# A decoder layer on one core: all units in one chain, a third memory unit in seven products, later pairs of y

## The chip, the cores and the metric

The kernel runs on one core of one Trainium2 chip. The time is device microseconds of one execution, the median of several. The profile is one further execution, taken by the hardware profiler; its rows give times in microseconds from the start of its span. The engines are called PE (TensorE's products), PEld (TensorE's weight loads, which overlap the products), DVE (VectorE), ACT (ScalarE), POOL (GpSimd) and SP (SyncE, which here only issues transfers).

## What is computed

One hybrid decoder layer on 256 tokens of width 2048, in fp32:

```python
h = x
h = h + 0.5 * swiglu(rmsnorm(h), w1_gate, w1_up, w1_down)       # f1, D_FF = 5632
z = rmsnorm(h) @ w_in                                           # q, kv, v, u
y_a = spatial_gating(gelu(z_u), gelu(z_v))                      # chunk 128, 8 groups
y_b = window_attention_sinks(z_q, z_k, z_v)                     # window 128, 16 heads, 2 kv heads
h = h + concat(rmsnorm(y_a), rmsnorm(y_b)) @ w_out              # wo
h = h + cross_attention(rmsnorm(h), rmsnorm(mem), w_xq, w_xkv, w_xo)   # mv0 mv1 mk0 mk1, xq, xo
h = h + 0.5 * swiglu(rmsnorm(h), w2_gate, w2_up, w2_down)       # f2
out = rmsnorm(h)
```

The memory has 256 rows; its projection `w_xkv` has 4096 columns, which four units of 1024 columns compute: mk0 and mk1 (keys) and mv0 and mv1 (values).

## The kernel before

**Products in three passes.** Every fp32 operand a is split into a rounded part ah (type fp32r) and a rest al; a product a.b is then ah.bh + al.bh + ah.bl, three matmuls of 128x128 by 128x512. `split` (L147) does it: ScalarE casts (L148), VectorE subtracts (L149).

**Units and chunks.** A unit is 1024 columns of a weight matrix for all 256 tokens, so its output is four blocks of 128x512 in PSUM. It runs over chunks of 256 rows of the weights; the 256x256 block of the activations that belongs to a chunk is a "pair" (a class `Pair`, L172), transposed, with its gain applied, and split. `load` (L298) issues the transfer of a chunk's weights, 1 MB on SP's queue, into one of three buffers `raw`, and splits them into `wh` and `wl`, of which there are two buffers each. `Unit.multiply` (L349) issues the products (L363).

**Kinds.** A chunk of kind N takes eight block products in three passes, 24 matmuls. A chunk of kind S takes seven by a scheme of the Strassen-Winograd sort, 21 matmuls, and needs sums of the weight blocks (a tile `t`, L310 to L314, split into `th` and `tl`) and sums of the activation blocks (`fill`, L193). Kind C takes 24 with other intermediates, and stands among S chunks in a unit. `KINDS` = "CCSCSCSC" is the order in the gate units and in mv1 and mk0; mv0 and mk1 are eight N chunks. The unit of seven products keeps its partial sums P1, Q6, Q7 in the PSUM pool `trp`, which the transposes also use (four banks); the other sums lie in `acc` (four banks). `seven_early` and `seven_late` (L479, L487) make the four blocks from them. For wo and xo, `KINDS_O` gives the kinds of the pairs and `HALVES_O` the kinds of the chunks in each of the two halves.

**The order.** TensorE's instructions run in the order in which they are traced (`manual_schedule` for PE). The other engines' orders, and which buffer a tile gets and when, are planned by the framework: by the order of tracing as a priority (`high_priority` lifts it), and by when inputs and buffers are ready in the planner's own estimate of time. `push` (L426) traces the load of a chunk, then `flush` (L411) traces the products of the chunk pushed before, and what follows them (`post`: evictions). So a load is traced one chunk ahead of its products. `unit` (L440), `narrow_unit` (L450) and `seven_unit` (L496) end with `flush`, so the next unit's first load is traced behind all of their products and evictions; `gu_unit`, `added_unit` and the down units don't flush within their stage.

**Side work.** Transposes and small products of attention, gating and norms are written as generators. `multiply` calls `side_step` (L389) after every six matmuls; a step runs one ready generator to its next `yield n`, which makes it ready again n steps later. `until` and `have` (L398, L403) run generators at once where a result is needed. Side work is `held` during the S chunks of units that use all four `trp` banks, and spaced by three steps in `sparse` units.

**Stages, in order.** f1: one plain gate unit on x as it is (its rows come transposed from DRAM by `prep1`, L736, one pair per chunk; the norm's factor is applied afterwards), then ten gate units on normalized forms n1, then four down units. Then q, kv, v, u; then mv0, mv1, mk0, mk1; then wo, xq, xo; then f2 with eleven gate units and four down units. The windowed attention (`attend`, L861, two lanes) runs as side work in v, u and mv0, the gating in mv0, the forms of y (`y_pairs`, L976) where `YFORMS` says, counted in finished chunks of mk0 and mk1, and the memory attention (`attend_memory`, L1082) in xq and xo. The pairs of the normalized memory, mT (`pair_normalized`, L252), are made one per chunk of u. `next_norm` (L664) makes the pairs for the next stage out of h; for n4 it scales rows by the factor of the first half first (`scaled`, L690).

**Pools.** `fp` has 14 forms of high and low parts, `tmp` seven tiles of 128x512 (tag `s2`: raw blocks, temporaries), `mid` twelve of 128x1024. An instruction that writes a tile waits until its buffer's last reader is done.

The lines that set the order around the change are:

```python
def push(u, i, w, p, post=None, pieces=None):
    ...
        b = load(u.s, w, u.kinds[i], pieces)
    flush()
    pending.append((u, i, p, b, post))
```

Of the kernel before, what the change touches and what calls it, by code (L numbers as in the profile page):

```python
# [8 lines left out]
F32 = mybir.dt.float32  # L9
# [13 lines left out]
NG = D // 512  # L23

# [6 lines left out]
def layer_kernel(  # L31
# [23 lines left out]
    ctx.enter_context(tc.manual_schedule(engines={mybir.EngineType.PE}))  # L55
# [185 lines left out]
    def pair_from_dram(s, srcT, i, gcol, base=None, raw=None):  # L241
        if raw is None:
            raw = s2(s + "r").rearrange("p (k t) -> p k t", k=2)
            nc.sync.dma_start(raw, srcT[i * T:(i + 1) * T, :].rearrange("(k p) t -> p k t", p=P))
# [7 lines left out]
    def pair_normalized(s, kind, srcT, i, gcol, by_token):  # L252

        raw = s2(s + "r").rearrange("p (k t) -> p k t", k=4)
        src = srcT[i * T:(i + 1) * T, :].rearrange("(k p) t -> p k t", p=P)
        for tb in range(TB):
            a, b = laid(kind, 0, tb), laid(kind, 1, tb)
            nc.gpsimd.dma_start(raw[:, a:b + 1:b - a, :], src[:, :, tb * P:(tb + 1) * P])
        turned = 1 if kind == "S" else 0
# [38 lines left out]
    def load(s, w, kind, pieces):  # L298
# [5 lines left out]
        if kind == "S":  # L304
# [4 lines left out]
            split(wh[:, 1:, :], wl[:, 1:, :], raw[:, 1:, :])  # L309
# [4 lines left out]
            nc.vector.tensor_tensor(t[:, 3, :], t[:, 2, :], raw[:, 3, :], ALU.add)  # L314
            split(th, tl, t)
# [95 lines left out]
    def flush():  # L411
        while pending:
            u, i, p, b, post = pending.pop(0)
            if u.late and all(name in u.left for name in u.late):
                held[0] = u.kinds.index("S") <= i <= u.kinds.rindex("S")
            held[0] = held[0] or i in u.alone
            tight[0] = u.sparse and u.kinds.index("S") <= i <= u.kinds.rindex("S")
            u.multiply(u.kinds[i], p(), b, i in (0, len(u.kinds) - 1))
            held[0] = False
# [4 lines left out]
    emptied = []  # L424

    def push(u, i, w, p, post=None, pieces=None):  # L426
        with ExitStack() as order:
            if emptied:

                order.enter_context(tc.issue_after(emptied.pop().ins))  # L430
            b = load(u.s, w, u.kinds[i], pieces)
        flush()
        pending.append((u, i, p, b, post))
# [3 lines left out]

    BLOCKS = (("P2", 0, 0), ("Q3", 0, 1), ("R", 1, 1), ("Q4", 1, 0))
# [11 lines left out]
    def narrow_unit(s, w, pairs):  # L450

        ps = [acc.tile([P, 512], F32, tag="acc", name=nm(s)) for _ in range(TB)]
        for c in range(2):
# [5 lines left out]
            for k in range(8):  # L459
                p = have(pairs, (c * 8 + k) // 2)  # L460
                side_step()
                for tb in range(TB):
                    hi, lo = p[f"A{tb + 1}{k % 2 + 1}"]
                    for i, (x, y) in enumerate(((hi, wh), (lo, wh), (hi, wl))):
                        nc.tensor.matmul(
                            ps[tb][:, :256], x, y[:, k, :],
                            start=c + k + i == 0, stop=c == 1 and k == 7 and i == 2,
                        )
        return ps

    KINDS = "CCSCSCSC"

    KINDS_O = "NNNSNSSN"
    HALVES_O = ("NNNNNNSN", "NNNSNSNN")
# [798 lines left out]
```

## Time and profile before

| | |
|---|---|
| median of 3 runs | 2106.76 us (2105.95 to 2106.78) |
| profiled execution, its own time | 2105.79 us |
| its span | 2104.0 us |
| granted clock, mean | 0.996 |
| moved by DMA | 402.15 MB, mean 191 GB/s |

The span is what the rows of the trace cover; the profiled execution's time is 1.8 us more. In the head of the page each engine has its busy time, its share of the span and its instructions. PE's products are pipelined and the ends of their rows are modelled, so rows overlap: what a product costs in a dense stretch is the distance from one start to the next. A row of windows gives the length of the stretch, then the busy time and number of instructions of PE, PEld, DVE, ACT and POOL, then the granted clock of TensorE (1.00 is full), the DMA's share and GB/s. A row of waits names who waited, for what, and then total, times and longest. A row of a timeline is start, length, engine, line, operation, output and inputs; in brackets stands the idle time before it and what ended it.

### The profile page before, as it was taken

What the parts mean: (1) busy time and instruction counts of PE and PEld (TensorE: products, weight loads), DVE (VectorE), ACT (ScalarE), POOL (GpSimd) and SP (SyncE); (2) the same over time, 40 slices, a digit from 0 to 9 for tenths busy, and PEclk for the clock granted to TensorE, in tenths of its full rate; (3) what the DMA queues carried; (4) which work ended last, traced back from release to release, by engine and by line L of the source; (5) the groups of instructions that cost most, each with busy time, mean ns of one, the idle gap of its engine ahead of it and who ended that gap; (6) DMA issues with size and microseconds to landing.
All of it is one profiled execution on the core that took longest, in us unless ns stands there. A gap on an engine that the chain in (4) does not pass through costs nothing.

```text
span 2104.0 us, 23815 instructions
## 1 busy us (share of the span) xinstructions
PE 2076.0 (99%) x9527; PEld 1715.5 (82%) x9527; DVE 1674.5 (80%) x1609; ACT 1135.4 (54%) x1109; POOL 32.2 (2%) x51
## 2 busy tenths in 40 slices
PE   9999999999999999999999999999999999999998
PEld 7888888888888888788888888778888888888886
DVE  5888888888987745867858657798888888889878
ACT  7655555555544645544545455665555545555444
POOL 0000000000000000100000000000000000000000
PEclk9999999999999999999999999999999999999999
DMA  7555555555555554435555543455555555555553
GB/s 281 195 189 213 200 195 184 209 188 199 202 199 206 201 210 166 167 140 200 180 180 184 197 160 140 163 197 200 181 207 197 204 191 200 200 200 200 200 198 122
DMA packets 60110, 402.15 MB, mean 191 GB/s; under 512 B 6864, under 2 KB 8928, under 8 KB 12768
## 3 DMA queue, kind: packets, MB, share of 16 engines
q1 hardware_dynamic: 57280, 393.50, 51.7%
q0 software_dynamic: 2016, 6.30, 0.9%
q8 instruction: 74, 1.21, 0.2%
q10 hardware_dynamic: 704, 0.84, 0.1%
q14 instruction: 36, 0.29, 0.0%
HBM read 398.52 MB, written 2.10 MB: 190 GB/s over the span
## 4 chain that ended last, share of the span: by engine, by line
PE 94%; DVE 3%; ACT 1%; issue 1%; DMA 1%; POOL 0%; SPq 0%; POOLq 0%; DVEq 0%; ACTq 0%
PE f2gQ L363 16%; PE f1gQ L363 15%; PE f1dQ L363 6%; PE f2dQ L363 6%; PE f2gP L363 6%; PE f1gP L363 5%; PE f1dP L363 3%; PE f2dP L363 3%; PE woQ L363 2%; PE xqQ L363 2%; PE f1dR L363 2%; PE f2dR L363 2%; PE xoQ L363 2%; PE mk0Q L363 1%; PE mv1Q L363 1%; PE mv0Q L363 1%
## 5 line engine op out<-in xcount | busy, mean ns | idle before, releaser
L149 DVE TENSOR_TENSOR f1gwl<-f1gw,f1gwh 128x2048 fp32r<-128x2048 f32 (+1 forms) x91 | 185.5, 2043 | 51.6 <-ACT f1gwh L148 51.4
L148 ACT CAST f2gwh<-f2gw 128x1536 fp32r<-128x1536 f32 (+1 forms) x88 | 154.4, 1755 | 133.4 <-PE f2gQ L363 96.6
L148 ACT CAST f1gwh<-f1gw 128x2048 fp32r<-128x2048 f32 (+1 forms) x91 | 156.1, 1716 | 123.5 <-PE f1gQ L363 90.4
L149 DVE TENSOR_TENSOR f2gwl<-f2gw,f2gwh 128x1536 fp32r<-128x1536 f32 (+1 forms) x88 | 183.7, 2088 | 40.3 <-ACT f2gwh L148 40.2
L363 PE MATMUL f2gQ<-f2gwh,n4fh 128*128 128x512 f32 x363 | 141.4, 390 | 0.0
L363 PE MATMUL f2gQ<-f2gwh,n4fl 128*128 128x512 f32 x363 | 141.3, 389 | 0.0
L363 PE MATMUL f1gQ<-f1gwh,n1fh 128*128 128x512 f32 x330 | 128.6, 390 | 0.0
L363 PE MATMUL f1gQ<-f1gwh,n1fl 128*128 128x512 f32 x330 | 128.4, 389 | 0.0
L148 ACT CAST f2dwh<-f2dw 128x2048 fp32r<-128x2048 f32 (+1 forms) x44 | 79.2, 1799 | 91.2 <-PE f2dQ L363 71.2
L148 ACT CAST f1dwh<-f1dw 128x2048 fp32r<-128x2048 f32 (+1 forms) x44 | 79.2, 1799 | 87.9 <-PE f1dQ L363 68.2
L149 DVE TENSOR_TENSOR f2dwl<-f2dw,f2dwh 128x2048 fp32r<-128x2048 f32 (+1 forms) x44 | 94.4, 2145 | 27.0 <-ACT f2dwh L148 24.3
L363 PE MATMUL f2gQ<-f2gwl,n4fh 128*128 128x512 f32 x363 | 115.7, 392 | 0.0
L149 DVE TENSOR_TENSOR f1dwl<-f1dw,f1dwh 128x2048 fp32r<-128x2048 f32 (+1 forms) x44 | 94.3, 2144 | 26.8 <-ACT f1dwh L148 24.2
L363 PE MATMUL f1gQ<-f1gwl,n1fh 128*128 128x512 f32 x330 | 105.1, 392 | 0.0
L149 DVE TENSOR_TENSOR f2gtl<-f2gt,f2gth 128x2048 fp32r<-128x2048 f32 x33 | 75.6, 2292 | 17.0 <-ACT f2gth L148 16.6
L149 DVE TENSOR_TENSOR f1gtl<-f1gt,f1gth 128x2048 fp32r<-128x2048 f32 x30 | 68.8, 2292 | 18.3 <-ACT f1gth L148 18.0
L363 PEld LDWEIGHTS f2gQ<-f2gwh,n4fl 128*128 128x128 f32 x363 | 68.1, 188 | 14.2
L363 PEld LDWEIGHTS f2gQ<-f2gwh,n4fh 128*128 128x128 f32 x363 | 68.2, 188 | 14.1
L363 PEld LDWEIGHTS f2gQ<-f2gwl,n4fh 128*128 128x128 f32 x363 | 67.3, 188 | 13.5
L148 ACT CAST f2gth<-f2gt 128x2048 fp32r<-128x2048 f32 x33 | 63.1, 1913 | 23.1 <-DVE f2gt L314 18.3
L363 PEld LDWEIGHTS f1gQ<-f1gwh,n1fl 128*128 128x128 f32 x330 | 62.0, 188 | 12.9
L363 PEld LDWEIGHTS f1gQ<-f1gwh,n1fh 128*128 128x128 f32 x330 | 62.0, 188 | 12.8
(703 smaller groups left out, 5715.1 us busy)
## 6 DMA issues: line engine op xcount, KB each, us to landing
f2gw<-in_w_gu SPq DMA_DIRECT2D x88, 1024.0 KB, 4.8
f1gw<-in_w_gu SPq DMA_DIRECT2D x87, 1024.0 KB, 4.8
f1dw<-in_w_down SPq DMA_DIRECT2D x44, 1024.0 KB, 4.8
f2dw<-in_w_down SPq DMA_DIRECT2D x44, 1024.0 KB, 4.8
wow<-in_w_out SPq DMA_DIRECT2D x16, 1024.0 KB, 4.8
xqw<-in_w_xq SPq DMA_DIRECT2D x16, 1024.0 KB, 4.8
xow<-in_w_xo SPq DMA_DIRECT2D x16, 1024.0 KB, 4.8
qw<-in_w_in SPq DMA_DIRECT2D x8, 1024.0 KB, 5.0
```

The costliest lines, as they stand in the source:

```text
L148: nc.scalar.copy(hi, src)
L149: nc.vector.tensor_tensor(lo, src, hi.bitcast(F32), ALU.subtract)
L363: nc.tensor.matmul(self.banks[name], x, y, start=name not in self.begun, stop=self.left[name] == 0)
```

## The change

**One chain.** Every unit now hands its evictions to `push` as a `post`, and none ends with `flush`; there is one `flush` at the end of f2. So the first load of a unit is traced ahead of the last products of the unit before. What was done ahead of a chunk's load (memory squares, memory pairs, forms) becomes `beside`, traced behind the chunk's load and ahead of the products of the chunk before. `unit`, `narrow_unit` and `seven_unit` take `late` functions (`late_q`, `late_kv`, `late_v`, `late_u`, `late_mv0`, `late_mk`, `late_xq`). The rule that held the load behind the plain unit's gates (`emptied`, `issue_after`) and the one that kept the table load in order are gone.

**mk1 in seven products**, as mk0. `KINDS_O` and the first of `HALVES_O` move one S kind: pair 6 becomes N, and the first half's S chunk is chunk 5, not 6. `YFORMS` counts wo's chunks too, and all forms of y are made from mk1 on.

**Memory**: the pair of chunk i is loaded by `beside` of u's chunk i + 1 and formed at i + 2, so the last two fall into mv0. v's scaling by its norm (L960) moves to u's chunk 2; the squares of v come behind its four evictions.

**The start**: `prep1` issues the next block of rows one chunk ahead; the squares of x come at chunks 3 and 4, the scaled rows of n1 at chunks 5, 6, 7, 7 (before 4, 5, 6, 7).

**f1 and f2**: the sums `t` of the weights are traced ahead of the split of the weights. The last gate unit fills three pairs ahead of the down units, not six; the down units fill the next pair and, at N chunks, one more. n4's first scaled rows wait two side steps.

The diff, cut:

```diff
+PINNED = {mybir.EngineType.PE}
-    ctx.enter_context(tc.manual_schedule(engines={mybir.EngineType.PE}))
+    ctx.enter_context(tc.manual_schedule(engines=PINNED))
...
             tl = stream.tile([P, 4, 512], F32R, tag="tl", name=nm(s + "tl"), bufs=1)
-            split(wh[:, 1:, :], wl[:, 1:, :], raw[:, 1:, :])
             nc.vector.tensor_tensor(
                 t[:, 0:2, :], raw[:, 1:3, :], raw[:, 0:1, :].to_broadcast([P, 2, 512]), ALU.add
             )
             nc.vector.tensor_tensor(t[:, 2, :], t[:, 0, :], raw[:, 2, :], ALU.add)
             nc.vector.tensor_tensor(t[:, 3, :], t[:, 2, :], raw[:, 3, :], ALU.add)
+            split(wh[:, 1:, :], wl[:, 1:, :], raw[:, 1:, :])
             split(th, tl, t)
...
+    def turn(run, post):
+        flush()
+        pending.append((run, post))
...
+    def push(u, i, w, p, post=None, pieces=None, beside=None):
+        b = load(u.s, w, u.kinds[i], pieces)
+        if beside is not None:
+            beside(i)
+        def run():
...
+            u.multiply(u.kinds[i], p(), b, i in (0, len(u.kinds) - 1))
+            held[0] = False
+        turn(run, post)
...
-    def unit(s, w, cb, pairs, beside=None):
+    def unit(s, w, cb, pairs, late, beside=None):
         u = Unit(s, "N" * 8)
         for i in range(8):
-            if beside is not None:
-                beside(i)
-            push(u, i, w[i, cb], lambda i=i: have(pairs, i))
-        flush()
-        return {(tb, j): u[name] for name, tb, j in BLOCKS}
+            push(
+                u, i, w[i, cb], lambda i=i: have(pairs, i),
+                (lambda: late({(tb, j): u[name] for name, tb, j in BLOCKS})) if i == 7 else None,
+                beside=beside,
+            )
...
-    KINDS_O = "NNNSNSSN"
-    HALVES_O = ("NNNNNNSN", "NNNSNSNN")
+    KINDS_O = "NNNSNSNN"
+    HALVES_O = ("NNNNNSNN", "NNNSNSNN")
...
-    def seven_unit(s, w, cb, pairs, dst):
-        u = Unit(s, KINDS, sparse=True)
+    def seven_unit(s, w, cb, pairs, dst, late=None):
+        u = Unit(s, KINDS_M, sparse=True)
+        until(lambda: len(attended) == 2 * TB)
...
-                for ahead in seq[at:at + 7]:
-                    inner(ahead)
                 at += 1
+                def ahead(q, at=at, kinds=kinds):
+                    inner(seq[min(at, len(seq) - 1)])
+                    todo = [j for j in seq[at + 1:at + 7] if pairs[j] is None]
+                    if kinds[q] == "N" and todo:
+                        inner(todo[0])
...
                     st["est"] = rstd_of(parts[:, :, :2], 2, 1024)
-                    for i in range(2):
-                        scaled(i)
+                    def first():
+                        yield 2
+                        for i in range(2):
+                            scaled(i)
+                    side_add(first())
...
+        raw = ahead.pop()
+        if i < 7:
+            ahead.append(s2("n0r").rearrange("p (k t) -> p k t", k=2))
+            nc.sync.dma_start(ahead[0], rows_of(xT, i + 1))
+        if i == 2:
+            blocks_of_x(2)
+        n0.append(pair_loaded("n0", raw, i, G_FFN1, [t[:, i % 2] for t in quad]))
+        if i == 1:
+            blocks_of_x(0)
+        for j in {3: (0, 1), 4: (2, 3)}.get(i, ()):
+            for tb in range(TB):
+                square_into(parts1[:, tb, j:j + 1], h[:, tb, j * 512:(j + 1) * 512], 512)
...
+        for j in {5: (0,), 6: (1,), 7: (2, 3)}.get(i, ()):
+            normalized(j)
...
+    def beside_u(i):
+        if i == 2:
+            for tb in range(TB):
+                nc.vector.scalar_tensor_tensor(
+                    out=v[tb], in0=v[tb], scalar=rsv[0][:, tb:tb + 1], in1=gv, op0=ALU.mult, op1=ALU.mult
+                )
+        beside_mT(i)
+    def beside_mT(i):
+        if loaded:
+            mT[i - 2] = pair_normalized("mT", KINDS_M[i - 2], loaded.pop(), i - 2, G_MEM, by_token)
+        if 1 <= i <= 8:
+            loaded.append(load_blocks("mT", KINDS_M[i - 1], memT, i - 1))
...
-    YFORMS = (2, 3, 5, 7, 8, 10, 12, 13)
+    YFORMS = (9, 10, 11, 16, 16, 17, 17, 18)
...
-            while chunks_done.get("mk0", 0) + chunks_done.get("mk1", 0) < YFORMS[k0 + i]:
+            while sum(chunks_done.get(n, 0) for n in ("mk0", "mk1", "wo")) < YFORMS[k0 + i]:
...
     for cb in range(2):
-        kr = [[s2("mk") for _ in range(TB)] for _ in range(2)]
-        if cb == 0:
-            seven_unit("mk0", w_xkv, 0, mT, lambda tb, j: kr[j][tb])
-        else:
-            pk = unit("mk1", w_xkv, 1, mT)
-            with tc.high_priority():
-                for name, tb, j in BLOCKS:
-                    nc.scalar.copy(kr[j][tb], pk[tb, j])
-        for j in range(2):
-            side_add(memory_keys(2 * cb + j, kr[j]))
+        kr, late_mk = key_rows(cb)
+        seven_unit(f"mk{cb}", w_xkv, cb, mT, lambda tb, j, kr=kr: kr[j][tb], late_mk)
...
-    tc.keep_in_program_order(silu_table())
-    flush()
+    silu_table()
...
     ffn("f2", lambda i: have(n4, i), rs4_, w2_gu, w2_down, on_final)
+    flush()
```

More of the change, by code (lines that the diff above doesn't have):

```diff
@@ L258, in pair_normalized @@
             nc.gpsimd.dma_start(raw[:, a:b + 1:b - a, :], src[:, :, tb * P:(tb + 1) * P])
+        return raw
+    def pair_normalized(s, kind, raw, i, gcol, by_token):
         turned = 1 if kind == "S" else 0
@@ L412, in flush @@
         while pending:
[L413 to L419, printed above, removed]
+            run, post = pending.pop(0)
+            run()
             if post is not None:
@@ L589, in gated @@
                 )
-            return last
         def inner(i):
@@ L734, in layer_kernel @@
     quad = []
+    ahead = [raw0]
     def prep1(i):
@@ L935, in attend @@
             attended.append(n)
-    for lane in range(2):
-        side_add(attend(lane))
     wst = m4("wst")
@@ L965, in layer_kernel, with late_u @@
     ny = [None] * 8
-    pu = unit("u", w_in, 0, n2, lambda i: mT.append(pair_normalized("mT", KINDS[i], memT, i, G_MEM, by_token)))
-    with tc.high_priority():
+    def late_u(pu):
+        rs2 = rs2_()
         for name, tb, j in BLOCKS:
```

246 lines of the change are left out of this document (137 added, 109 removed).

## The prediction

> **What bounds the kernel now.** I read the head of the profile's page first.
>
> ```profile
> span 2104.0 us, 23815 instructions
> PE 2076.0 (99%) x9527; PEld 1715.5 (82%) x9527; DVE 1674.5 (80%) x1609; ACT 1135.4 (54%) x1109; POOL 32.2 (2%) x51
> ```
>
> TensorE is busy for all but 28.0 us, so a change can gain only in three ways: fewer products, fewer pauses, or less time at a low clock. The last 24 us come next, by windows (columns: length, then busy time of PE, PEld, DVE, ACT, POOL, then the granted clock).
>
> ```profile
> 2080.00:2100.00 20.00, 13.72 (x61) 11.04 (x59) 16.11 (x26) 6.23 (x11) 1.92 (x2) 0.89 0.16 59
> 2100.00:2104.00 4.00, 0.00 (x0) 0.00 (x0) 0.00 (x0) 0.00 (x0) 0.00 (x0) 0.50 0.60 228
> ```
>
> The tail, which the change doesn't touch, takes 6.28 + 4.00 = 10.3 of the 28.0 us. So 17.7 us of pauses are left. The list of TensorE's waits names most of them (total, times, longest):
>
> ```profile
> PE wop L918 <- DVE pTs L913: 4.8, 2, 4.6
> PE f1gP L363 <- DVE n0l L143: 1.9, 1, 1.9
> PE n L218 <- ACT n4s L693: 1.4, 2, 1.1
> PE f2dQ L363 <- DVE f2dtl L149: 1.2, 2, 0.6
> PE f2gQ L363 <- DVE f2gtl L149: 1.1, 2, 0.6
> PE xoP L363 <- DVE xofl L149: 1.0, 1, 1.0
> PE xoP L363 <- DVE xowl L149: 0.8, 1, 0.8
> PE xoP L363 <- ACT xofh L148: 0.7, 1, 0.7
> PE xoQ L363 <- DVE h L514: 0.7, 1, 0.7
> PE f1gP L363 <- ACT n0h L142: 0.6, 1, 0.6
> PE f1gQ L363 <- DVE f1gtl L149: 0.6, 1, 0.6
> ```
>
> Two of these cost more than they show. After them the clock stands at half:
>
> ```profile
> 40.00:42.00 2.00, 1.05 (x3) 0.86 (x4) 2.00 (x5) 0.00 (x0) 0.00 (x0) 0.72 1.11 405
> 42.00:44.00 2.00, 2.00 (x9) 1.60 (x7) 0.23 (x1) 0.00 (x0) 0.00 (x0) 0.50 0.98 345
> 44.00:46.00 2.00, 2.00 (x13) 1.70 (x11) 0.76 (x2) 1.66 (x4) 0.00 (x0) 0.92 0.76 293
> 850.00:852.00 2.00, 1.96 (x9) 1.84 (x9) 1.52 (x3) 0.51 (x2) 0.38 (x1) 0.50 0.96 391
> 852.00:854.00 2.00, 2.00 (x6) 1.16 (x5) 1.88 (x6) 0.10 (x1) 1.06 (x2) 0.50 0.30 80
> 854.00:856.00 2.00, 2.00 (x6) 1.61 (x6) 1.59 (x5) 0.99 (x4) 0.00 (x0) 0.50 0.20 57
> 856.00:858.00 2.00, 2.00 (x9) 1.59 (x8) 0.00 (x0) 1.95 (x2) 0.00 (x0) 0.83 0.00 0
> ```
>
> The loss is the length times (1 - clock): 0.56 + 1.00 + 0.16 = 1.7 us near 42 us, and 1.00 + 1.00 + 1.00 + 0.34 = 3.3 us near 853 us. Everything the change could win lies in these lists, plus the products that it removes.
>
> **The third memory unit in seven products (mk1).** Eight N chunks of 24 products become five chunks of 24 and three of 21, so nine products go. Their price, from the chain of waits:
>
> ```profile
> 100.58 4.08 PE f1gQ L363 x18
> ```
>
> 4.08 / 18 = 0.227 us each, so 9 x 0.227 = 2.0 us, all of it on TensorE's path. What it adds lies on VectorE: three sets of sums and their splits, and the seven-product evictions (seven on VectorE) in place of four ScalarE copies. The cover is TensorE's own 41 us in that unit. Its neighbour of the same form, mv1, shows that the cover holds:
>
> ```profile
> 960.00:980.00 20.00, 20.00 (x90) 16.57 (x89) 17.48 (x13) 9.86 (x7) 0.00 (x0) 1.00 0.58 211
> ```
>
> VectorE is at 17.48 of 20 there and TensorE doesn't pause. Without the cover each S chunk waits as `f2gtl` does, 0.6 us, and three of them eat 1.8 of the 2.0. The later y forms take VectorE work out of mk1. They are needed only from the first chunks of wo. By the code's step counter (one side step per six products, 1.36 us) the last of them starts about 14 steps into wo, while the S chunk that forces it comes after 20. I cost this at nothing. If it slips, the price is again a forced chain of the `xofh` + `xofl` kind, 1.7 us. The moved S kind leaves the number of products in wo and xo as it was.
>
> **The start.** The first unit's pause has this chain:
>
> ```profile
> 17.38 14.78 SPq L323 DMA_DIRECT2D f1gw<-in_w_gu  x4
> 32.21 0.43 SPq L244 DMA_DIRECT2D n0r<-in_xT  x1
> 38.02 0.90 ACT L142 ACTIVATE n0h<-n0r,sm 128x256 fp32r<-128x256 f32 x2
> 40.41 0.88 DVE L143 SCALAR_TENSOR_TENSOR n0l<-n0r,sm,n0h 128x256 fp32r<-128x256 f32 x2
> 40.95 0.79 PE L363 MATMUL f1gP<-f1gwh,n0l 128*128 128x512 f32 x1 [1.87 <-DVE n0l L143]
> ```
>
> The rows of x-transposed for chunk 5 are issued on SP only behind four weight loads, at 32.21, and their split comes 6 to 8 us later. The new `prep1` asks for each block one chunk (8 x 3 x 0.227 = 5.4 us) earlier, ahead of the temporaries of the n1 forms, and starts those forms one chunk later. SP's traced order of the loads doesn't change otherwise: the two x blocks still stand ahead of chunk 2's weights, the other two ahead of chunk 3's. So the pauses before chunks 1 to 3 stay. Gain if cured: 0.6 + 1.9 idle + 1.7 clock = 4.2 us; if the pause only moves, 0. I take 4.2, since 5.4 us of lead is twice the 2.5 us that were missing.
>
> The clock dropped here after 0.6 and 1.9 us of idleness. [...]
>
> **The u unit.** The largest pause:
>
> ```profile
> 835.92 0.60 PE L909 MATMUL pT<-ident,scs 128*128 128x128 f32 x4
> 841.26 2.48 DVE L960 SCALAR_TENSOR_TENSOR v<-v,rs,gv 128x1024 f32<-128x1024 f32 x2 [0.84 <-POOL rs L133]
> 843.66 0.88 DVE L263 SCALAR_TENSOR_TENSOR mTr<-mTr,sm,by_token 128x256 f32<-128x256 f32 x2
> 844.91 2.28 DVE L149 TENSOR_TENSOR uwl<-uw,uwh 128x2048 fp32r<-128x2048 f32 x1
> 849.30 0.68 DVE L913 COPY pTs<-pT 128x512 f32<-128x512 f32 x1
> ```
>
> The attention's transposes end at 836.5, and VectorE copies them out at 849.30: the scaling of v, two memory pairs and a weight split are queued ahead of the copy. The change moves the scaling to u's chunk 2 and memory pair i from chunk i to chunk i + 2, so in chunks 0 and 1 the copy has only weight splits ahead of it. In chunk 2 its queue is 2.48 + 2.3 (split) + about 2.4 (pair) = 7.2 us, against five side steps, 5 x 1.36 = 6.8 us, plus the inserted work. That is enough by a hair. Gain if cured 4.6 + 3.3 = 7.9; if the queue only comes two chunks later, 0. I take 7.9. Memory pairs run into mv0's chunk 1, ahead of need. Their transfers stand on GpSimd's queue with the small powers; u's gate needs those only after u. The attention must be complete before mv1's load, which is now traced before mv0's last chunk, four side steps earlier.
>
> ```profile
> 947.81 1.00 PE L918 MATMUL wop<-kv,pTs 128*128 128x64 f32 x8
> 951.47 0.39 PE L363 MATMUL mv0P<-mv0wh,mTfh 128*128 128x512 f32 x1
> ```
>
> Its last product starts at 947.81, mv0's last chunk at 951.47, so it ends two steps ahead of even that, and nothing is forced.
>
> **xo and the norms.** The S chunk of wo's and xo's first half comes one chunk earlier, so its nine additions leave VectorE before the unit's evictions (the `h` wait, 0.7), and the scaled rows of n4 start two side steps sooner than their transposes (the `n4s` wait, 1.4): 2.1 us. If ScalarE is late by as much again, 0. On the other side the S chunk now follows head 3's product at once and needs its PSUM banks: that is among the new waits below.
>
> **Sums of weights before splits, fewer forms in the last gate unit.** The waits on `tl` are 1.2 + 1.1 + 0.6 = 2.9 us. The sums depend on the load alone, so moving them ahead lets ScalarE split them sooner; but VectorE's total is unchanged. Between 0 and 2.9 I take 1.5.
>
> **One chain.** Loads of a unit's first chunk are traced before the last products of the unit before. Their transfers were issued ahead already (three buffers), and the list of waits has no pause at the joins of plain units. So: 0. Dropped order rules (the table load, the load behind the gates) are 0 too, under TensorE's products.
>
> **New waits.** About eight places are re-ordered (start, kv, v to u, u to mv0, mk1, wo, xo, down units). The trace of before can't show them. From below 0; from above one pause of the `wop` kind with its clock, 7.9. I take half the places at 0.6 to 1.4 us, like most rows of the list: 4.0 us.
>
> **The sum.** -2.0 - 4.2 - 7.9 - 2.1 - 1.5 + 4.0 = -13.7 us. The profiled execution took 2105.8 (span 2104.0 and 1.8 around it), and the median of the three runs, 2106.76, stands 1.0 above that. So the span becomes 2090.3, the profiled time 2092.1, the median 2093.
>
> **The rivals.**
>
> All cured, nothing new. For it: each cure has its row. Against: VectorE's 80% leaves little room. The 4.0 go and the other 1.4 of `tl` come: 2106.8 - 2.0 - 4.2 - 7.9 - 2.1 - 2.9 = 2087.7.
>
> The u pause moves. For it: 7.2 us of queue against 6.8. Against: the other inserted work lengthens the steps. 2093 + 7.9 = 2101.
>
> The start's pause moves to the n1 forms. They need VectorE beside the splits, one chunk nearer to their use. Against: by the counter each is made three chunks ahead. 2093 + 4.2 = 2097.
>
> The change doesn't do what it says: the planner of ScalarE and VectorE orders by readiness, so the traced order matters little, and only mk1's 2.0 us come, eaten in part by new waits: 2105 to 2107.
>
> Slower: the joins. These rows are ScalarE at the join of v and u:
>
> ```profile
> 834.22 0.68 ACT L956 ACTIVATE v<-vR,rs 128x512 f32<-128x512 f32 x1
> 834.79 1.90 ACT L148 CAST uwh<-uw 128x2048 fp32r<-128x2048 f32 x1
> 837.21 0.68 ACT L956 ACTIVATE v<-vQ,rs 128x512 f32<-128x512 f32 x1
> ```
>
> A weight cast already stands ahead of the last eviction. If earlier loads put a cast that waits for the last chunk's buffer ahead of the first eviction, the next unit gets no bank until 1.9 + 0.7 us after the last product: a 2.6 us pause, enough for the clock by the row at 40.95, with 1.7 more. At eight joins that is 34 us, so 2093 + 34 = 2127; it decides from four joins on. Against: the first bank is complete three quarters of a chunk, 4.1 us, before the unit's end, and the new v unit takes its four evictions ahead of the squares. [...]
>
> **How the numbers follow.** Forecast 2093: 0.38. All cured: 0.15. The u pause moves: 0.17. The start's moves: 0.11. Nothing but mk1: 0.10. Slower joins: 0.09. A measurement of this kernel tells 0.2%, 4.2 us, from no change, so faster is below 2102.5: the forecast, all cured, the start's, and two thirds of the u case, 0.38 + 0.15 + 0.11 + 0.11 = 0.75. Within 0.2%: the rest of the u case and most of the fourth, 0.14. Slower: 0.11. The range reaches from all cured with half of the two `xof` waits gone too (2084) to just over no change (2108).
>
> **What would show it.** TensorE's product count falls by 9. `wop <- pTs` and `f1gP <- n0l` leave the list of waits, and no window holds a clock of 0.50 outside the first and last microseconds. `n <- n4s` goes. TensorE's idle time outside the tail falls from 17.7 to about 13 us or less. If a 0.50 window stands in u or mv0, the queue only moved; a pause at the first product of a unit shows the slower rival; a VectorE wait in mk1 shows the cover gone.

## The result, and the profile after

The median falls from 2106.36 us (four runs beside it, 2104.54 to 2106.78) to 2082.24 us (four runs, 2082.10 to 2082.59). The ratio is 0.9887, with a 95% interval of 0.9870 to 0.9905. The kernel is 24.1 us faster; the forecast was 13.7 us, and its range ended 1.8 us too high.

The profiled execution took 2082.59 us, 1.7 us more than its span. This is the head of the page of the kernel after:

```profile
span 2080.9 us, 23813 instructions
PE 2065.4 (99%) x9518; PEld 1712.7 (82%) x9518; DVE 1684.6 (81%) x1621; ACT 1137.1 (55%) x1104; POOL 30.2 (1%) x51
```

The span is 23.1 us shorter; the medians lie 1.0 us further apart, because the profiled execution stands 0.6 us below the median of the kernel before and 0.4 us above that of the kernel after. Nine products are gone, as said. VectorE works 10.1 us more than before in a shorter span, so nothing was won by giving it less to do. TensorE is idle for 2080.9 - 2065.4 = 15.5 us. The tail is still 10.3 us, by a window of the kernel after:

```profile
2070.60:2080.90 10.30, 0.00 (x0) 0.00 (x0) 3.94 (x10) 2.27 (x6) 1.86 (x2) 0.68 0.54 204
```

So 5.2 us of idle time are left outside the tail, where 17.7 stood before. This is TensorE's list of waits after, as far as it names them (4.8 of the 5.2 us):

```profile
PE warm L99 <- DVE ones L90: 1.1, 1, 1.1
PE f1gP L368 <- ACT n0h L144: 0.8, 2, 0.4
PE xoP L368 <- ACT xofh L150: 0.7, 1, 0.7
PE f1gQ L368 <- DVE f1gtl L151: 0.6, 1, 0.6
PE n L220 <- DVE n2fl L145: 0.5, 1, 0.5
PE f2gQ L368 <- ACT f2gth L150: 0.4, 1, 0.4
PE f2gQ L368 <- DVE f2gtl L151: 0.3, 1, 0.3
PE xoP L368 <- DVE xofl L151: 0.2, 1, 0.2
PE f1gP L368 <- DVE n0l L145: 0.2, 1, 0.2
```

`wop <- pTs`, `n <- n4s`, `xoQ <- h`, `xoP <- xowl` and `f2dQ <- f2dtl` have left, and `xofl` falls from 1.0 to 0.2. The old pauses for `n0h` (0.6) and `n0l` (1.9) before chunk 5 are gone whole: what the list still has under these names lies in the first chunk and is new (0.41, 0.38 and 0.22 us; see the start below). No pause of more than about 0.4 us is new.

Where the 23.1 us lie is read from the first starts of each unit's products. These are rows by tile (shortest, median and longest duration in ns, then first and last start), first of the kernel before:

```profile
L363 PE MATMUL uQ<-uwh,n2fh x32: 389/389/794, 836.3 to 898.9; 128*128 128x512 f32 x32
L363 PE MATMUL mv0Q<-mv0wh,mTfh x32: 387/391/499, 903.1 to 956.2; 128*128 128x512 f32 x32
L363 PE MATMUL mk0Q<-mk0wh,mTfh x31: 389/389/476, 999.7 to 1041.1; 128*128 128x512 f32 x31
L363 PE MATMUL xoQ<-xowh,xofh x55: 389/389/497, 1282.8 to 1388.3; 128*128 128x512 f32 x55
L363 PE MATMUL f2gQ<-f2gwh,n4fh x363: 389/389/477, 1390.3 to 1858.4; 128*128 128x512 f32 x182
L363 PE MATMUL f2dQ<-f2dwh,f2afh x140: 389/389/395, 1860.4 to 2092.9; 128*128 128x512 f32 x140
```

The same rows of the kernel after:

```profile
L368 PE MATMUL uQ<-uwh,n2fh x32: 389/389/499, 831.8 to 885.9; 128*128 128x512 f32 x32
L368 PE MATMUL mv0Q<-mv0wh,mTfh x32: 387/391/499, 890.1 to 943.3; 128*128 128x512 f32 x32
L368 PE MATMUL mk0Q<-mk0wh,mTfh x33: 389/389/389, 986.8 to 1026.2; 128*128 128x512 f32 x33
L368 PE MATMUL xoQ<-xowh,xofh x55: 389/389/482, 1267.7 to 1368.5; 128*128 128x512 f32 x55
L368 PE MATMUL f2gQ<-f2gwh,n4fh x363: 387/389/482, 1370.5 to 1837.6; 128*128 128x512 f32 x182
L368 PE MATMUL f2dQ<-f2dwh,f2afh x140: 389/389/393, 1839.6 to 2069.7; 128*128 128x512 f32 x140
```

A stretch is the difference of two first starts; the last one runs to the end of the span.

| stretch | before | after | change | forecast |
|---|---|---|---|---|
| start of the span to u | 836.3 | 831.8 | -4.5 | -4.2 |
| u | 66.8 | 58.3 | -8.5 | -7.9 |
| mv0, mv1 | 96.6 | 96.7 | +0.1 | 0 |
| mk0, mk1, wo, xq | 283.1 | 280.9 | -2.2 | -2.0 |
| xo, with n4's first forms | 107.5 | 102.8 | -4.7 | -2.1 |
| f2's gate units | 470.1 | 469.1 | -1.0 | -1.5 with the next row |
| f2's down units, tail | 243.6 | 241.3 | -2.3 | |
| new waits, anywhere | | | none that a stretch shows | +4.0 |
| sum | | | -23.1 | -13.7 |

### The profile page after: what moved, and what is told of

It reads as the page before. It is cut to its first block, busy times and chain, and to the rows that moved or that the text cites. A ratio compares the mean times of both kernels' runs of the same rounds, so it can differ in the third digit from the quotient of the medians.

```text
span 2080.9 us, 23813 instructions
## 1 busy us (share of the span) xinstructions
PE 2065.4 (99%) x9518; PEld 1712.7 (82%) x9518; DVE 1684.6 (81%) x1621; ACT 1137.1 (55%) x1104; POOL 30.2 (1%) x51
## 4 chain that ended last, share of the span: by engine, by line
PE 97%; DVE 2%; ACT 1%; issue 0%; DMA 0%; POOLq 0%; POOL 0%; SPq 0%; DVEq 0%
PE f2gQ L368 16%; PE f1gQ L368 15%; PE f2dQ L368 6%; PE f1dQ L368 6%; PE f2gP L368 6%; PE f1gP L368 5%; PE f2dP L368 3%; PE f1dP L368 3%; PE woQ L368 2%; PE xoQ L368 2%; PE xqQ L368 2%; PE f2dR L368 2%; PE f1dR L368 2%; PE mk1Q L368 1%; PE mk0Q L368 1%; PE mv1Q L368 1%
## 5 line engine op out<-in xcount | busy, mean ns | idle before, releaser
L368 PEld LDWEIGHTS f1gQ<-f1gwh,n1fl 128*128 128x128 f32 x330 | 62.0, 188 | 12.8
L368 PEld LDWEIGHTS f1gQ<-f1gwh,n1fh 128*128 128x128 f32 x330 | 62.0, 188 | 12.8
```

The lines of the kernel that those rows point to most:

```text
L368: nc.tensor.matmul(self.banks[name], x, y, start=name not in self.begun, stop=self.left[name] == 0)
```

## How the cured pauses look

**The start.** Rows of the timeline of the kernel after; the chunk that waited at 38.58 before now starts at 37.49:

```profile
35.74 0.48 DVE L145 SCALAR_TENSOR_TENSOR n0l<-n0r,sm,n0h 128x256 fp32r<-128x256 f32 x1
...
37.81 0.39 PE L368 MATMUL f1gP<-f1gwh,n0l 128*128 128x512 f32 x1
```

The low parts are begun 2.1 us ahead of their product; before they were begun at 40.41 and the product waited for them until 40.95.

The first chunk has new waits instead. ScalarE makes the two halves of `n0h` one behind the other in the kernel before (6.12 us, 0.91 long); in the kernel after two casts of weights stand between them:

```profile
6.60 1.32 ACT L150 CAST f1gwh<-f1gw 128x512 fp32r<-128x512 f32 x2
7.82 0.50 ACT L144 ACTIVATE n0h<-n0r,sm 128x256 fp32r<-128x256 f32 x1
```

```profile
8.38 0.49 PE L368 MATMUL f1gP<-f1gwh,n0h 128*128 128x512 f32 x1 [0.38 <-ACT n0h L144]
```

Every kernel below that is built on the changed one has such waits there too; the two with the old order of the units, the one before and the one with the sums alone, have none. Which edit makes them is open. In this execution they came with a loss of clock, 0.34 + 1.00 + 0.36 = 1.7 us in the windows from 8 to 14 us. Yet chunk 4 begins at 31.70, where it began at 31.79 before: three waits for weights, of the kernel before, have left the list and took up the delay.

```profile
PE f1gP L363 <- ACT f1gwh L148: 1.1, 3, 0.6
```

With the early fills (below), whose code is the same up to here, the clock held (1.00 in the windows from 0 to 12 us), two of these waits stand (0.5 us), and chunk 4 begins at 31.28.

**The u unit.** VectorE's rows of the kernel after, at the join of v and u (a bracket gives the idle time before):

```profile
832.18 0.69 DVE L977 COPY pTs<-pT 128x512 f32<-128x512 f32 x1 [4.73 <-PE pT L973]
...
837.51 1.28 DVE L1030 SCALAR_TENSOR_TENSOR v<-v,rs,gv 128x1024 f32<-128x1024 f32 x1
```

VectorE stands idle when the transposes (831.48, 0.60 long) end and copies them out 0.1 us later, where it came 12.8 us after their end before. v's scaling comes behind that, in two parts with a weight split between them (the other starts at 842.34). The 7.2 us of queue in u's chunk 2, which I had feared to be too long by a hair, never stands as one block.

**The joins.** ScalarE's rows of the kernel after:

```profile
830.96 0.69 ACT L1018 ACTIVATE v<-vQ,rs 128x512 f32<-128x512 f32 x1
831.53 1.92 ACT L150 CAST uwh<-uw 128x2048 fp32r<-128x2048 f32 x1
```

The cast now stands behind v's last eviction, not ahead of it. The slower rival had it the other way round at eight joins; no join shows a pause.

**mk1.** A window of the kernel after shows that the cover held: VectorE busy for 15.94 of 20 us, TensorE without a pause.

```profile
1040.00:1060.00 20.00, 20.00 (x94) 16.54 (x93) 15.94 (x16) 10.46 (x10) 0.00 (x0) 1.00 0.60 208
```

## The experiments

Two theories stood against each other. Theory 1: each pause went with the edit that moved its own work, so undoing that edit alone brings back that pause and its price. Theory 2: the chain, with the new order of tracing that it gives the planner, moved the pauses, and the single edits do little. Unless another is named, each kernel is the changed one (2082.24 us, span 2080.9) with the one edit shown; the times are medians of four runs.

**The rows of x at their old time.**

```diff
-        raw = ahead.pop()
-        if i < 7:
+        if i:
             ahead.append(s2("n0r").rearrange("p (k t) -> p k t", k=2))
-            nc.sync.dma_start(ahead[0], rows_of(xT, i + 1))
+            nc.sync.dma_start(ahead[0], rows_of(xT, i))
+        raw = ahead.pop()
```

> The changed kernel, with the rows of x-transposed asked for in the chunk that uses them, not one chunk ahead. Theory 1 (each pause went with the edit that moved its own work): the pause near 41 us and its low clock come back, 4.4 us, so about 2086.6. Theory 2 (the gain comes from joining the units in one chain, which gives the planner another order everywhere): 2083 or less.

2086.01 us (2085.21 to 2087.08), ratio to the kernel before 0.9909 (0.9894 to 0.9923): 3.8 us given back. Waits of this kernel:

```profile
PE f1gP L368 <- DVE n0l L145: 4.2, 5, 1.8
```

`n0l` is back, now 4.2 us in five pauses, where the profile of before had 1.9 in one. They are not where I expected them: the largest stand at 15.72 (1.63) and 47.94 (1.82), not near 41, and in this execution the clock held (1.00 in the windows from 6 to 16 and from 42 to 50 us). The start isn't cured without the earlier request.

**n1's scaled rows one chunk sooner, as before.**

```diff
-        for j in {5: (0,), 6: (1,), 7: (2, 3)}.get(i, ()):
+        for j in {4: (0,), 5: (1,), 6: (2,), 7: (3,)}.get(i, ()):
```

> The changed kernel, with the scaled rows of n1 at chunks 4, 5, 6, 7 as before; the rows of x-transposed are still asked for one chunk ahead. If the earlier request alone cured the start, within 0.5 us of 2082.2; if the later forms were needed too, a pause for n0's low part near 40 us, up to 4 us, so up to 2086.

2085.62 us (2084.68 to 2086.46), ratio 0.9906 (0.9891 to 0.9921): 3.4 us given back. The timeline of this kernel shows the pause at another place than expected, the transposes of n1; behind it the clock is 0.66 from 35 to 40 us, with products 0.43 us apart (36.33 and 36.76) instead of 0.227:

```profile
34.74 0.33 PE L220 MATMUL n<-ident,n1s 128*128 128x128 f32 x1 [3.13 <-ACT n1s L799]
```

Both edits of the start are needed: without the one the split of x is late, without the other ScalarE's rows of n1. The two prices don't add up to the 4.5 us that the start won; each is that of a pause which the other edit alone would leave.

**Memory pairs at their old chunk, the chain kept.**

```diff
-        if loaded:
-            mT[i - 2] = pair_normalized("mT", KINDS_M[i - 2], loaded.pop(), i - 2, G_MEM, by_token)
-        if 1 <= i <= 8:
-            loaded.append(load_blocks("mT", KINDS_M[i - 1], memT, i - 1))
+        if i < 8:
+            mT[i] = pair_normalized("mT", KINDS_M[i], load_blocks("mT", KINDS_M[i], memT, i), i, G_MEM, by_token)
```

> The changed kernel, with memory pair i loaded and formed beside chunk i of u as before, not at i + 2; v's scaling stays at u's chunk 2. Theory 1: a pause of 4 to 5 us before a product of the attention and half the clock after it come back in u, about 8 us, so 2089 to 2091. Theory 2: 2084 or less.

2087.96 us (2087.35 to 2091.97), ratio 0.9922 (0.9907 to 0.9936): 5.7 us given back. But the pause is another one, on ScalarE's exponentials, in the timeline of this kernel:

```profile
857.53 0.93 PE L973 MATMUL pT<-ident,scs 128*128 128x128 f32 x4 [2.85 <-ACT scs L964]
```

ScalarE in turn had waited 3.61 us for VectorE, which masks the scores of this step at 854.97, behind a weight split and a memory form; in the changed kernel it does so at 849.22.

**The same, with v's scaling at chunk 1 too.**

```diff
-        if i == 2:
+        if i == 1:
...
+        if i < 8:
+            mT[i] = pair_normalized("mT", KINDS_M[i], load_blocks("mT", KINDS_M[i], memT, i), i, G_MEM, by_token)
```

> The changed kernel, with both parts of u undone as far as the new chain allows: memory pair i beside chunk i, v's scaling at chunk 1. Undoing the pairs alone gave 5.7 us. If v's scaling holds the rest of u's 8.5 us, about 2090.5; if the scaling's place is worth nothing, 2088.

2087.56 us (2086.31 to 2091.29), ratio 0.9921 (0.9904 to 0.9937), with the same 2.85 us pause and no `wop <- pTs` of over 0.4 us. The moved work does stand ahead of the copy again. In the timeline of this kernel the transposes end at 832.00, v's scaling, a weight split and a memory pair come first, and the copy is 8.4 us late:

```profile
840.38 0.68 DVE L977 COPY pTs<-pT 128x512 f32<-128x512 f32 x1
```

TensorE had other products up to nearly then: its wait for the copy is 0.17 us. The next run undoes the whole.

**All of u as before**: the chain cut ahead of u, pairs and scaling ahead of the loads, the squares between v's evictions.

```diff
+        if s == "u":
+            flush()
         for i in range(8):
+            if s == "u":
+                beside(i)
...
-                beside=beside,
+                beside=None if s == "u" else beside,
...
-        if i == 2:
+        if i == 0:
...
+        if i < 8:
+            mT[i] = pair_normalized("mT", KINDS_M[i], load_blocks("mT", KINDS_M[i], memT, i), i, G_MEM, by_token)
```

> The changed kernel, with the whole of u as before: the chain cut ahead of u, memory pairs and v's scaling traced ahead of the loads of chunks 0 to 7, v's squares between its evictions. If the 8.5 us of u are the queue in front of the attention's copies, the wait of 4.6 us and the low clock after it come back: u 8 us longer, 2090 to 2091. If undoing the memory pairs already gave all that u's order is worth (4.2 us in its profile), 2086 to 2088, and the rest of the 8.5 us came from elsewhere.

2091.58 us (2090.61 to 2091.86), ratio 0.9931 (0.9916 to 0.9946): 9.3 us given back, 0.6 above what I expected. u is 68.0 us long again (831.4 to 899.4 by its rows). The transposes end at 831.68, and the copy now has a second weight split and a second memory pair ahead of it, 12.8 us in all. It and the pause, in the timeline of this kernel:

```profile
844.46 0.68 DVE L981 COPY pTs<-pT 128x512 f32<-128x512 f32 x1
```

```profile
845.19 1.97 PE L986 MATMUL wop<-kv,pTs 128*128 128x64 f32 x8 [4.56 <-DVE pTs L981]
```

And the windows behind it, of the same kernel:

```profile
846.00:854.00 8.00, 8.00 (x22) 5.98 (x22) 4.14 (x12) 3.89 (x7) 1.44 (x2) 0.50 0.25 91
854.00:856.00 2.00, 2.00 (x9) 1.63 (x8) 1.33 (x1) 0.77 (x3) 0.00 (x0) 0.89 0.00 0
```

The pause of 4.56 is back, and a loss of clock with it that is larger than before: 4.00 + 0.22 = 4.2 us from 846 on, against 3.3. That is the largest term of the sum, shown. Either the chain or the moved work alone keeps this pause away: the two kernels shown last, and the next one, don't have it, though with the chain alone the copy is late and the other pause, of 2.85, comes. Of the kernels run, only the one with both undone has the pause of 4.56.

**The chain cut at every join, all else kept.**

```diff
     def unit(s, w, cb, pairs, late, beside=None):
+        flush()
...
     def narrow_unit(s, w, pairs, late, beside):
+        flush()
...
     def seven_unit(s, w, cb, pairs, dst, late=None):
+        flush()
...
     def added_unit(s, w, cb, pairs, on_block):
+        if cb == 0:
+            flush()
...
     def ffn(s, get, rs, wgu, wd, on_block, first=None):
+        flush()
```

> The changed kernel, with the chain cut again at the end of every unit and stage: the next unit's first load is traced behind the last products and evictions. Theory 1: within 1 us of 2082.2, since the list of waits of the kernel before has no pause at the joins. Theory 2: most of the gain is lost, 2095 or more.

2084.29 us (2083.78 to 2084.36), ratio 0.9899 (0.9883 to 0.9916): 2.0 us given back, at one place, in the timeline of this kernel:

```profile
898.98 1.16 PE L1085 MATMUL sv<-v,wst 128*128 128x128 f32 x8 [1.15 <-DVE u L1092]
```

The gating's products in mv0 wait for VectorE's product of the gate with u. Undone as the only edit, the chain is worth 2.0 of the 24.1 us; theory 2 falls as the main cause, and so does my price of nothing for the chain.

**mk1 in eight N chunks.**

```diff
-        seven_unit(f"mk{cb}", w_xkv, cb, mT, lambda tb, j, kr=kr: kr[j][tb], late_mk)
+        if cb == 0:
+            seven_unit("mk0", w_xkv, 0, mT, lambda tb, j, kr=kr: kr[j][tb], late_mk)
+        else:
+            unit("mk1", w_xkv, 1, mT, late_mk)
```

> The changed kernel, with mk1 as eight N chunks again; the forms of y stay late. Both theories: nine products more at 0.227 us, 2.0 us, so 2084.2. If VectorE's work in the seven products had cost TensorE anything, less than 2.0.

2084.38 us (2084.29 to 2084.47), ratio 0.9901 (0.9886 to 0.9915): 2.1 us, beside 9 x 0.227 = 2.0. No wait is new in mk1.

**The old kinds of wo and xo.**

```diff
-    KINDS_O = "NNNSNSNN"
-    HALVES_O = ("NNNNNSNN", "NNNSNSNN")
+    KINDS_O = "NNNSNSSN"
+    HALVES_O = ("NNNNNNSN", "NNNSNSNN")
```

> The changed kernel, with the old kinds for wo and xo: pair 6 in S form again, the first half's S chunk at chunk 6. Theory 1: the 0.7 us wait for the evictions at xo's middle comes back, and one S form more is made in wo and in xo, so 0.7 to 1.7 us, 2083 to 2084. If the S chunk right behind head 3's product costs as much as was feared, nothing or a gain.

2084.81 us (2083.79 to 2085.64), ratio 0.9900 (0.9883 to 0.9916): 2.6 us by the median, 1.2 in the profiled execution. The stretch of xo is 1.7 longer there (104.5 us), and that is the price to go by: of the four runs two took 2083.8 and 2084.1 us at a mean clock of 0.998, two 2085.5 and 2085.6 at 0.997. Two waits of this kernel are back at the size that they had before:

```profile
PE xoP L368 <- DVE xofl L151: 1.0, 1, 1.0
...
PE xoQ L368 <- DVE h L537: 0.7, 1, 0.7
```

I had put `h` to this edit, but not `xofl`: I took the two `xof` pauses for fixed.

**n4's first rows at once.**

```diff
-                    def first():
-                        yield 2
-                        for i in range(2):
-                            scaled(i)
-                    side_add(first())
+                    for i in range(2):
+                        scaled(i)
```

> The changed kernel, with n4's first rows scaled at once, not two side steps later. Theory 1: the wait of n4's transposes for ScalarE comes back, 1.4 to 1.8 us, so 2083.6 to 2084. Theory 2 (the wait went because the S chunk moved and VectorE is free sooner): within 0.5 us of 2082.2.

2084.81 us (2084.64 to 2085.10), ratio 0.9899 (0.9884 to 0.9913): 2.6 us, above the 1.4 to 1.8 expected. Waits of this kernel:

```profile
PE n L220 <- ACT n4s L721: 1.4, 2, 1.1
...
PE xoP L368 <- DVE xowl L151: 0.7, 1, 0.7
```

`n4s` returns, as forecast, and `xowl` with it. The split of xo's last weights is a row of VectorE, in the timeline of this kernel and then of the changed one:

```profile
1364.42 2.28 DVE L151 TENSOR_TENSOR xowl<-xow,xowh 128x2048 fp32r<-128x2048 f32 x1
```

```profile
1357.55 2.29 DVE L151 TENSOR_TENSOR xowl<-xow,xowh 128x2048 fp32r<-128x2048 f32 x1
```

In the changed kernel it is ahead of the unit's evictions; here ScalarE's cast before it is 1.8 us later (1357.37 instead of 1355.60), seven evictions of 0.6 us each have gone ahead on VectorE, and the split is 6.9 us later. It is the pause of the u unit in small: work that is not urgent ahead of work that is.

**The sums of the weights behind the split again.**

```diff
+            split(wh[:, 1:, :], wl[:, 1:, :], raw[:, 1:, :])
             nc.vector.tensor_tensor(
                 t[:, 0:2, :], raw[:, 1:3, :], raw[:, 0:1, :].to_broadcast([P, 2, 512]), ALU.add
             )
...
-            split(wh[:, 1:, :], wl[:, 1:, :], raw[:, 1:, :])
```

> The changed kernel, with the sums of the weights traced behind the split of the weights again. Theory 1: the waits on the split sums come back where VectorE is full, 1.5 to 3 us, so 2083.7 to 2085.2. Theory 2 (the planner orders VectorE by readiness, so the traced order of two ready things hardly matters): within 0.5 us of 2082.2.

2088.21 us (2088.11 to 2088.28), ratio 0.9915 (0.9900 to 0.9929): 6.0 us, the dearest single edit after u and twice the most that I expected. Waits of this kernel:

```profile
PE f2dQ L368 <- DVE f2dtl L151: 1.2, 2, 0.6
PE f1dQ L368 <- DVE f1dtl L151: 1.2, 2, 0.6
```

f2's down units take 243.6 us again (241.3 in the changed kernel), f1's 237.5 instead of 235.2, and xo 1.4 more. A pair of pauses that the list gives at 1.2 us costs 2.3 in the stretch.

**The kernel before with that order alone.** The edit is made to the kernel before.

```diff
-            split(wh[:, 1:, :], wl[:, 1:, :], raw[:, 1:, :])
...
             nc.vector.tensor_tensor(t[:, 3, :], t[:, 2, :], raw[:, 3, :], ALU.add)
+            split(wh[:, 1:, :], wl[:, 1:, :], raw[:, 1:, :])
```

> The kernel before, with one part of the change alone: the sums of the weights traced ahead of the split of the weights. If the order of these two is worth what the last runs say (6.0 us when it is undone in the changed kernel), 4 to 6 us faster than before, most of it in the down units, in the last gate units and in xo. If it is worth that only beside the new fills, 2 us or less.

2103.64 us (ten runs, 2101.85 to 2105.05) beside 2105.81 (13 runs): ratio 0.9990 (0.9981 to 0.9999). The span is 2101.5, 2.5 less, and f2's down units take 241.2 instead of 243.6, so all of it lies there. This edit is worth 2.2 by the medians when made alone and 6.0 as the last one: in the kernel before f1's down units had no such pause (235.1 and 235.2 us with the two orders).

**The fills of the down units as before.**

```diff
-                        rs() if (c, i) == (0, 5) else inner(i - 5) if c == 10 and i >= 5 else None
+                        rs() if (c, i) == (0, 5) else inner(i - 2) if c == 10 and i > 1 else None
...
-                    inner(seq[min(at, len(seq) - 1)])
-                    todo = [j for j in seq[at + 1:at + 7] if pairs[j] is None]
-                    if kinds[q] == "N" and todo:
-                        inner(todo[0])
+                    for j in seq[at - 1:at + 6]:
+                        inner(j)
```

> The changed kernel, with the fills as before: six pairs filled in the last gate unit, seven ahead in the down units. Theory 1: the waits for split sums in the last gate unit and in the down units come back, four of 0.6 to 0.8 us, so 2084.5 to 2085.5. Theory 2: these went with the traced order of the sums, so within 0.5 us of 2082.2, and the run with the sums traced later carries them.

2082.23 us (2082.16 to 2082.59), ratio 0.9887 (0.9872 to 0.9901): no difference. The fills are worth nothing here.

**Sums and fills as before**, both edits above.

```diff
+            split(wh[:, 1:, :], wl[:, 1:, :], raw[:, 1:, :])
...
+                    for j in seq[at - 1:at + 6]:
+                        inner(j)
```

> The changed kernel, with both the sums behind the split and the fills as before. The sums alone undone cost 6.0 us, of which 2.3 in f1's down units, where the kernel before had no such waits. If the old order is bad there only beside the new fills, this run is 2 us faster than that one, about 2086; if not, 2088.

2088.15 us (2088.10 to 2088.25), ratio 0.9916 (0.9899 to 0.9932), as with the sums alone. So the fills aren't what makes the old order dearer in the changed kernel's f1. What does is open.

**Two versions beyond the change.** What is left in xo is the split of the attention's result. First the forms of n2 and n3 two steps apart, and the memory attention's last stage one step sooner:

```diff
-                    yield 4 if i % 2 == 0 and mixed else 1
+                    yield 4 if i % 2 == 0 and mixed else 1 if mixed else 2
...
-        yield 4
+        yield 3
         for half in range(2):
```

> A try to beat the changed kernel: the memory attention's last product one side step sooner (a pause of 0.83 + 0.50 us at xo's chunk 4 should go), and the forms of n2 and n3 two side steps apart, not one (the pause of 0.70 us for a PSUM bank in f1's last down unit should go). 2080.2 if both go; a new pause in wo or xq, where n3's forms then come later, would give it back.

2081.73 us (2081.34 to 2081.93), ratio 0.9887 (0.9873 to 0.9902). The `n2fl` wait falls from 0.5 to 0.2, and `xofh` stays at 0.7: one step wasn't enough. With the stage before it one step sooner too:

```diff
-        yield 5
+        yield 4
         ptv = bank("xpT").rearrange("p (b t) -> p b t", b=2)
```

> A second try to beat the changed kernel: n2's and n3's forms two steps apart and the memory attention's last two stages one step sooner each. If the last product of head 2 is thereby traced ahead of xo's chunk 4, its pause of 0.83 + 0.50 us goes: 2080.4. If ScalarE's exponentials are then late for the transposes, another pause of 1 us or more takes its place.

2081.22 us (2080.99 to 2081.78), ratio 0.9883 (0.9868 to 0.9898). `xofh` and `xofl` have left the list; one new wait stands in it, of the transposes `xpT` for VectorE's `pr`, 0.6 us in two pauses.

Its four runs all lie below the changed kernel's four, by 0.3 us at the nearest, and its median by 1.0. It beats the kernel before clearly; against the changed one the ratios' intervals overlap, and the gain rests on those runs and on a span of 2079.5.

No run undid the later forms of y or the dropped order rules alone.

## Why the prediction was wrong

The direction was right, every cure that it booked whole came, and u, the start and mk1 had nearly the size forecast. The sum was 9.4 us short (23.1 in the span against 13.7). Taking away the new waits alone would not have been enough: the rival without them, with every `tl` wait cured, gains 19.1 us, and 2.6 of the other 4.0 lie in xo. By its own steps:

- **New waits, +4.0: failed, and the largest miss.** I took eight re-ordered places, half of them with a pause of a common size. None came that is over about 0.4 us; the only ones at a re-ordered place, 1.0 us in the first chunk with 1.7 of clock, are made good by chunk 4. The runs show why such an average misleads: with the chain cut there is one (1.15 us in mv0), with the memory pairs early under the chain another (2.85), with n1's rows early a third (3.13). The places are real, and another edit of the same change keeps each of them clear. The "all cured" rival, which had no new waits, said 2087.7 and was nearer.
- **xo, -2.1: the mechanism right, the size wrong, by 2.6.** I counted two waits as gone, and four went: with `h` (0.7) and `n4s` (1.4) also `xofl` (0.8 of 1.0), which the kinds carry, and `xowl` (0.8), which n4's delay carries. Idle time of 0.7 + 1.4 + 0.8 + 0.8 = 3.7 us became 4.7 us of stretch.
- **The sums ahead of the splits, -1.5: mis-sized, by 1.8.** f2 won 3.3. "VectorE's total is unchanged" was true and beside the point: the waits were of order, not of load.
- **The u unit, -7.9: right.** 8.5 in the table and 9.3 by undoing it, with the pause back and its loss of clock longer. The step's "by a hair" compared one queue with five steps, though the planner cut that queue in two.
- **The start, -4.2: right in the pause, with some luck in the sum.** 4.5 in the table; either half undone costs 3.4 to 3.8. But "the pauses before chunks 1 to 3 stay" failed: they are gone from the profile after, and the new waits of the first chunk stand against them at nearly the same price.
- **mk1, -2.0: right,** at 2.1 by undoing it. The later forms of y at nothing: the table's stretch from mk0 through xq holds mk1's gain whole, and no cost of theirs shows in it; no run undid them alone.
- **One chain, 0: wrong by 2.0 as a part,** though the sum didn't suffer by it: without the chain the changed kernel has a wait that the kernel before didn't have.

The differences in the table add up to 4.0 + 2.6 + 1.8 + 0.6 + 0.3 + 0.2 - 0.1 = 9.4.

The rivals: neither the pause of u nor that of the start moved on; the planner of ScalarE and VectorE does follow the traced order, since the kernel with the sums alone changes that order only and moves f2 by 2.4 us; the joins didn't stall. One expectation failed: a window at clock 0.50 was not to stand outside the first and last microseconds, and one stands at 10 us (below).

The prices of undoing single edits (3.8, 3.4, 9.3, 2.0, 2.1, 2.6, 2.6, 6.0) add up to 31.8, more than the change won. They are prices of the last edit, not shares.

## What to carry to other kernels

Where one engine is at 99% and its waits can be listed, each wait whose work the change moves ahead of its need can be booked at its full row, with its clock, and also its neighbours that stand in the same queue behind the same late instruction. An allowance for unnamed new waits is worth no more than the place and the row that it can be given; without them it belongs in the range, not in the forecast. Undo edits one at a time, but don't read the prices as shares: edits that cover each other's holes cost more singly than together.

## What was not expected of the hardware

**The listed pauses were a floor.** Products' rows are 0.39 to 0.50 us long at a spacing of 0.227, so by these lengths the first 0.16 us or more of a delay lies under the row before. In the kernel with the sums behind the split, two products of f1's down units start 0.99 us apart (619.63 and 620.62), 0.76 above the spacing, and the list gives 0.60. The stretches show more than the list in four places: listed 3.7, stretch 4.7 (xo); listed 1.2, stretch 2.3 (f1's down units with the old sums); listed 1.4 + 0.7, stretch 2.7 (n4 at once); listed 0.8 + 0.7, stretch 1.7 (old kinds). Only part of the difference is settled by the hidden 0.16 us each.

**The clock's drop didn't follow from the pause's length.** The kernel before lost its clock after idle times of 0.59 and 1.87 us. With the rows late, the timeline shows nearly the same two:

```profile
45.62 0.49 PE L368 MATMUL f1gP<-f1gwh,n0h 128*128 128x512 f32 x1 [0.59 <-ACT n0h L144]
47.94 0.50 PE L368 MATMUL f1gP<-f1gwh,n0l 128*128 128x512 f32 x1 [1.82 <-DVE n0l L145]
```

Yet the window behind them, of the same kernel, is at full clock:

```profile
48.00:50.00 2.00, 2.00 (x11) 1.68 (x12) 1.07 (x3) 2.00 (x4) 0.00 (x0) 1.00 0.71 188
```

In the profiled executions the pause of 2.85 us cost the clock with the memory pairs early (0.68, then 0.50, in the windows from 858 to 862 us) and nothing with v's scaling early too (1.00 there). And the changed kernel lost it in its first chunks, by these windows of it (0.82 in the next one):

```profile
6.00:8.00 2.00, 1.56 (x6) 0.62 (x5) 1.29 (x4) 1.72 (x4) 0.00 (x0) 1.00 0.96 212
8.00:10.00 2.00, 1.41 (x4) 0.90 (x5) 1.93 (x4) 1.87 (x5) 0.00 (x0) 0.83 1.09 448
10.00:12.00 2.00, 2.00 (x6) 1.60 (x5) 0.59 (x2) 0.35 (x2) 0.00 (x0) 0.50 0.98 380
```

That is 10 products and 1.03 us idle in 4 us. The kernel with the early fills, whose code is the same there, had 9 products and 1.39 us idle in the same 4 us, and kept its clock at 1.00 there. So the same or more idleness went either way between these executions, and what decides it is not shown. The times spread with the clock: the four runs of the kernels with the 2.85 us pause lie 4.6 and 5.0 us apart, the longest of each at a mean clock of 0.995 and the others at 0.997 to 0.999; those of the changed kernel lie 0.5 apart, at 0.998 and 0.999.
